# Hybrid trunk: the recurrence's block inversion from 8x8 blocks instead of 16x16, with one more level of doubling on TensorE

## The chip, the core and the metric

One core of one Trainium2 chip runs the whole layer in one launch. The metric is device time in microseconds (us). In the text, PE is TensorE (PEld its weight loads), DVE VectorE, ACT ScalarE, POOL GpSimd and SP SyncE, which here only issues transfers. The engines run their own instruction streams in order and wait for each other with semaphores.

## The reference, cut to what matters

One layer over 256 latent and 256 context tokens, width 2048: a recurrent branch (16 heads of 64, forward and backward), a convolution branch, gates, an output projection, then 16 routed experts. The change lies in the recurrence alone:

```python
def step(S, inp):                       # per head, S is 64x64
    r_t, k_t, v_t, w_t, kk_t, a_t = inp
    sa = jnp.einsum('bhvk,bhk->bhv', S, kk_t)
    S = (S * w_t[:, :, None, :] - sa[..., None] * (kk_t * a_t)[:, :, None, :]
         + v_t[..., None] * k_t[:, :, None, :])
    y = jnp.einsum('bhvk,bhk->bhv', S, r_t) if emit else None
    return S, y
```

The kernel does not step through tokens. It cuts a sequence into chunks of 64 tokens and turns a chunk into matrix products. For that it needs, per chunk and head, the inverse of a 64x64 triangular matrix with a unit diagonal: identity plus the masked products of kk with kk*a.

## The kernel before, in words

**Stages of the trace.** Up to 577 us the input projections and the convolution run. From 577 to 1262 us the recurrence runs, then until 1320 us what is left of the gates, then two projections, and from about 1490 us the experts, whose weights (about 400 MB) come in at the memory's speed to the end. The tiles that hold the first expert weights reuse the recurrence's space, so all of that starts after it.

**The recurrence** works on 16 units: eight pairs of heads, each in two directions. A unit's code is a generator in five segments. Segment 1 makes decays and scaled operands (mostly ACT, POOL and DVE). Segment 2 makes the scores (PE L729, masked by DVE into `AT` at L731 and into `KM` at L734) and transposes `VK` and `KB` on PE (L740). Segment 3 is the inversion. Segment 4 applies the inverse (L857) and forms chunk-to-chunk operators in two PSUM banks, which DVE reads out as `PT` and `RB` (L881, L883). Segment 5 chains the chunks (L890 to L904: PE and ACT in turn) and gives `y`. A hand-written table `ORD` interleaves five units: inversion of unit i+1, segment 4 of unit i, scores of unit i+2, segment 1 of unit i+3, segment 5 of unit i.

**The inversion** handles a unit's 16 matrices (8 chunks, 2 heads) at once, 32x32 blocks on the diagonal first. ACT copies those blocks into `Ab`. DVE selects the 16x16 diagonal blocks with two masked additions into `INP` (L781, L783), transposes to `N` (L785) and does a forward substitution of 14 steps, each a product into `tmp` (L792 or L797, by direction) and an addition into `N` (L800). It transposes back (`OUT` L802), spreads the result (`TT` L805) and transposes it (`T` L808). One level of block doubling makes 32x32 inverses of it: PE multiplies the off-diagonal part `X` (masked by POOL, L777) with `T` (L813: 32 small products, four quadrants of the array side by side), ACT copies to `Q`, PE multiplies with `TT` (L820), DVE subtracts from `T` (L822) and transposes (L824). A second doubling, to 64x64, follows on PE and ACT (L833, L842, into `NT8`); the change does not touch it.

**Filling.** The gates' projections (products L221 to L223 into the PSUM bank "big", 12 for each 256 KB of weights that SP loads as `wraw`, ACT rounds as `whi` and POOL completes as `wlo`, L217) and the modulation products (L271) are handed out to the 16 units by `fills`, at lower priority. A scheduler, with times of its own, sets the order of every engine when the program is built. Filling that finds no place in the recurrence stands behind it.

**Buffers.** Segment 3 takes its tiles from rings: `t1` (three of 8x32 elements), `t2` (three of 16x32), `INP` (one).

Of the kernel before, what the change touches and what calls it, by code (L numbers as in the profile page):

```python
# [86 lines left out]
_n = 0  # L87
for _name, _w in (("ident", 128), ("bones", 128), ("ones", 128), ("mA", 128), ("mM", 128),
                  ("d1", 520), ("iota", 32),
                  ("mq", 2), ("mh", 2), ("ml2", 2), ("id16", 16), ("m16", 64), ("sel", 2), ("selE", 16), ("hsel", 2)):  # L90
    _CON[_name] = (_n, _n + _w)
    _n += _w
NCON = _n
# [2 lines left out]
def shape_constants():  # L96
    c = np.zeros((128, NCON), np.float32)
    p = np.arange(128)

    def put(name, v):  # L100
        a, b = _CON[name]
        c[:, a:b] = v.reshape(128, b - a)

    put("ident", np.eye(128))
    put("bones", (p[:, None] // 64 == p[None, :] // 64) * 1.0)
    put("ones", np.ones((128, 128)))
    s = (p % 64)[:, None]
# [4 lines left out]
    l2 = (p % 32) // 16
    put("ml2", (l2[:, None] == np.arange(2)) * 1.0)
    put("mq", (l2[:, None] == np.arange(2)) * -1.0)
    put("id16", ((p % 16)[:, None] == np.arange(16)) * 1.0)
    m16 = [(l2[:, None] == d) & (np.arange(32)[None, :] // 16 == 1 - d) for d in range(2)]
# [12 lines left out]
def kernel(  # L129
# [179 lines left out]
    with tc.tile_pool(name="st", bufs=1) as st:  # L309
# [52 lines left out]
    with tc.tile_pool(name="p1", bufs=1) as p1:  # L362
# [261 lines left out]
    def rwkv_dir(p, d, Pv, bonr, bon, INP):  # L624
# [148 lines left out]
        Ab8 = rt("Ab", "t1", [8, 32])  # L773
        for z, r in quads:
            act_copy(Ab8[r].rearrange("p (c h) t -> p c h t", h=2), par(AT[r], 1 - z // 2)[..., 32 * (z % 2):32 * (z % 2) + 32])
        X = rt("X", "t1", [8, 32])
        POOL.tensor_tensor(X, Ab8, cst("m16")[:, d * 32:d * 32 + 32][:, None, :].to_broadcast([128, 8, 32]), op=OP.mult)  # L777

        mq, mh, ml2 = cst("mq"), cst("mh"), cst("ml2")
        sel = INP.rearrange("p x u -> p u x")[:, 0:8]  # L780
        DVE.scalar_tensor_tensor(sel, Ab8[:, :, 0:16], mq[:, 0:1], cst("id16")[:, None, :].to_broadcast([128, 8, 16]),  # L781
                                 op0=OP.mult, op1=OP.add)
        DVE.scalar_tensor_tensor(sel, Ab8[:, :, 16:32], mq[:, 1:2], sel, op0=OP.mult, op1=OP.add)  # L783
        N = rt("N", "t2", [16, 32])
        DVE.transpose(N, INP)  # L785
        Nv = N.rearrange("p x (l y) -> p l x y", l=2)
        for j in range(1, 15):
            n, m = j, 15 - j
            tmp = rt("tmp", "tmp", [2 * 56])[:, 0:2 * n * m]
            if d == 0:  # L790
                tv = tmp.rearrange("p (l r s) -> p l r s", l=2, r=m)
                DVE.tensor_tensor(tv, Nv[:, :, j:j + 1, 0:j].to_broadcast([128, 2, m, n]),  # L792
                                  Nv[:, :, j + 1:16, j:j + 1].to_broadcast([128, 2, m, n]), op=OP.mult)
                o = Nv[:, :, j + 1:16, 0:j]
            else:
                tv = tmp.rearrange("p (l s r) -> p l s r", l=2, r=m)
                DVE.tensor_tensor(tv, Nv[:, :, 0:j, j:j + 1].to_broadcast([128, 2, n, m]),  # L797
                                  Nv[:, :, j:j + 1, j + 1:16].to_broadcast([128, 2, n, m]), op=OP.mult)
                o = Nv[:, :, 0:j, j + 1:16]
            DVE.tensor_tensor(o, o, tv, op=OP.add)  # L800
        OUT = rt("OUT", "t2", [16, 32])
# [3 lines left out]
        DVE.tensor_tensor(TT.rearrange("p u (l x) -> p u l x", l=2), outv[:, :, None, :].to_broadcast([128, 8, 2, 16]),  # L805
                          ml2[:, None, :, None].to_broadcast([128, 8, 2, 16]), op=OP.mult)
        T = rt("T", "t1", [8, 32])
        DVE.transpose(T, TT)  # L808
        pq = c8(bank("sb"))
        for i in range(8):  # L810
            tick(0.12)
            for z, r in quads:
                mark["X"] = PE.matmul(pq[r, i, 0:32], X[r, i], T[r, i], start=True, stop=True)  # L813
        Q = rt("Q", "t1", [8, 32])
        act_copy(Q, pq[:, :, 0:32])
        pq = c8(bank("sb"))
        for i in range(8):
            tick(0.12)
            for z, r in quads:
                PE.matmul(pq[r, i, 0:32], TT[r, i], Q[r, i], start=True, stop=True)  # L820
        T2 = rt("T2", "t1", [8, 32])
        DVE.tensor_tensor(T2, T, pq[:, :, 0:32], op=OP.subtract)  # L822
        TT = rt("TT", "t1", [8, 32])
        DVE.transpose(TT, T2)  # L824
# [557 lines left out]
```

## Time and profile before

| what | value |
|---|---|
| median of 3 runs (lowest, highest) | 2432.16 us (2431.11, 2433.72) |
| the profiled execution's own time, and its span | 2433.61 us, 2431.8 us |
| PE busy over the span | 2006.9 us (83%) |
| DVE busy | 1023.9 us (42%) |
| ACT, POOL busy | 763.2 us (31%), 650.8 us (27%) |
| granted PE clock over the span | 0.901 of full speed |
| chain that ended last, over the span: DMA, PE, DVE | 31%, 20%, 6% |

The shares over the span average stages with different limits: transfers at 427 GB/s set the last 900 us, and DVE is hardly busy there. The rows further down are therefore cut to the recurrence. The clock column (PEclk) is a mean of two levels, 1.0 (2.4 GHz) and 0.5 (1.2 GHz). Idle time in front of an instruction carries the name of what ended it.

### The profile page before, as it was taken

How to read it: one execution, taken by the hardware profiler on the slowest of the kernel's cores; microseconds unless marked ns; L12 is line 12 of the kernel's file. 1: busy time of each engine (PE TensorE's matmuls, PEld its weight loads, DVE VectorE, ACT ScalarE, POOL GpSimd, SP SyncE). 2: the span in 40 equal slices, each digit the busy share in tenths (PEclk: the TensorE clock that was granted, in tenths of full speed). 3: DMA queues.
4: the chain of work that ended last, by engine and by line, in shares of the span. 5: the costliest groups of instructions: out<-in, count | busy, mean ns of one | idle time of the engine just before them, and what ended most of it. 6: DMA issues, size and time to landing. Idle time of an engine off the chain costs nothing.

```text
span 2431.8 us, 45085 instructions
## 1 busy us (share of the span) xinstructions
PE 2006.9 (83%) x18730; PEld 1415.9 (58%) x18730; DVE 1023.9 (42%) x2029; ACT 763.2 (31%) x1524; POOL 650.8 (27%) x690
## 2 busy tenths in 40 slices
PE   7998999996877989988798996877777777777765
PEld 3787888894755877767678994433333333333332
DVE  2337888426777787665601543211111111111112
ACT  3254333634545565556443541000000000000002
POOL 1342333336433545445445732000000000000002
PEclk9999999998778999999998998888889889888987
DMA  9958666665213334234256887999999999999995
GB/s 384 343 183 271 216 218 233 202 213 181 60 56 109 125 123 139 96 134 152 97 197 198 280 314 303 427 427 428 428 427 427 428 427 429 427 428 427 428 416 221
DMA packets 145932, 669.94 MB, mean 275 GB/s; under 512 B 17344, under 2 KB 40000, under 8 KB 108608
## 3 DMA queue, kind: packets, MB, share of 16 engines
q1 hardware_dynamic: 128208, 455.49, 50.9%
q10 hardware_dynamic: 17520, 211.58, 20.6%
q8 instruction: 147, 2.41, 0.4%
q14 instruction: 57, 0.47, 0.1%
HBM read 647.28 MB, written 19.73 MB: 274 GB/s over the span
## 4 chain that ended last, share of the span: by engine, by line
DMA 31%; PE 20%; DVE 6%; ACT 3%; POOL 2%; issue 2%; SPq 0%; ACTq 0%; DVEq 0%; POOLq 0%
DMA wx<-in_w_gu 18%; DMA wx<-in_w_dn 10%; PE big L1261 2%; PE rw L1224 2%; DMA wraw<-in_w_in 2%; PE p L1293 2%; DVE N L800 1%; PE rw L1253 1%; PE big L221 1%; PE big L223 1%; PE rw L223 1%; PE big L222 1%; PE rw L221 1%; PE rw L222 1%; POOL wlo L217 1%
## 5 line engine op out<-in xcount | busy, mean ns | idle before, releaser
L217 POOL TENSOR_TENSOR wlo<-wraw,whi 128x512 fp32r<-128x512 f32 x292 | 394.4, 1356 | 517.4 <-ACT whi L146 450.0
L1261 PE MATMUL big<-wx,xse 128*32 128x512 f32 x2048 | 300.1, 721 | 160.3 <-DMA wx<-in_w_gu 158.4
L146 ACT ACTIVATE whi<-wraw 128x512 fp32r<-128x512 f32 x428 | 263.4, 627 | 420.2 <-DMA wraw<-in_w_in 130.0
L221 PE MATMUL big<-hh,whi 128*128 128x256 f32 x912 | 272.7, 299 | 13.6 <-ACT whi L146 6.1
L223 PE MATMUL big<-hh,wlo 128*128 128x256 f32 x912 | 271.0, 298 | 10.1 <-POOL wlo L217 9.9
L1261 PEld LDWEIGHTS big<-wx,xse 128*32 128x32 f32 x2048 | 63.8, 121 | 358.9 <-DMA wx<-in_w_gu 183.6
L222 PE MATMUL big<-hl,whi 128*128 128x256 f32 x912 | 268.1, 294 | 0.0
L1237 POOL TENSOR_TENSOR r<-r 128x256 f32<-128x256 f32 x11 | 8.2, 747 | 922.0 <-ACT r L1233 921.6
L221 PEld LDWEIGHTS big<-hh,whi 128*128 128x128 f32 x912 | 181.7, 199 | 40.0 <-issue 17.7
L223 PEld LDWEIGHTS big<-hh,wlo 128*128 128x128 f32 x912 | 181.6, 199 | 23.2 <-POOL wlo L217 14.1
L1274 ACT ACTIVATE th<-big 128x256 f32<-128x256 f32 x16 | 6.1, 384 | 584.9 <-PE big L1261 472.5
L222 PEld LDWEIGHTS big<-hl,whi 128*128 128x128 f32 x912 | 182.1, 200 | 7.4 <-issue 5.8
L1275 DVE SCALAR_TENSOR_TENSOR th<-th,big 128x256 f32<-128x256 f32 x16 | 6.7, 421 | 408.0 <-ACT th L1274 408.0
L1228 DVE SCALAR_TENSOR_TENSOR x<-rw,modT,x 128x256 f32<-128x256 f32 x256 | 111.3, 479 | 142.1 <-PE rw L1224 142.0
L217 DVE TENSOR_TENSOR wlo<-wraw,whi 128x512 fp32r<-128x512 f32 x136 | 112.7, 834 | 131.0 <-ACT whi L146 122.7
L1224 PE MATMUL rw<-oT,ye 128*128 128x256 f32 x512 | 132.4, 403 | 32.5 <-ACT ye L146 31.7
L223 PE MATMUL rw<-hh,wlo 128*128 128x256 f32 x512 | 149.9, 294 | 6.8 <-POOL wlo L217 6.8
L221 PE MATMUL rw<-hh,whi 128*128 128x256 f32 x512 | 150.3, 296 | 1.5 <-ACT whi L146 1.1
L222 PE MATMUL rw<-hl,whi 128*128 128x256 f32 x512 | 149.0, 293 | 0.0
L463 DVE SCALAR_TENSOR_TENSOR cv<-up,hcw,cv 128x256 f32<-128x256 f32 x240 | 144.6, 608 | 9.5 <-ACT cv L461 2.8
L1224 PEld LDWEIGHTS rw<-oT,ye 128*128 128x128 f32 x512 | 95.2, 196 | 85.9 <-ACT ye L146 72.4
L1253 PEld LDWEIGHTS rw<-oh,xk 128*128 128x128 f32 x1024 | 123.2, 194 | 34.2 <-issue 29.1
(359 smaller groups left out, 3901.4 us busy)
## 6 DMA issues: line engine op xcount, KB each, us to landing
wx<-in_w_gu ACTq DMA_DIRECT2D x66, 2048.0 KB, 39.2
wx<-in_w_gu SPq DMA_DIRECT2D x61, 2048.0 KB, 39.3
wm<-in_w_mod SPq DMA_DIRECT2D x96, 1024.0 KB, 7.2
wraw<-in_w_in SPq DMA_DIRECT2D x300, 256.0 KB, 4.2
wx<-in_w_dn ACTq DMA_DIRECT2D x32, 2048.0 KB, 38.6
wx<-in_w_dn SPq DMA_DIRECT2D x31, 2048.0 KB, 38.1
wraw<-in_w_o SPq DMA_DIRECT2D x64, 256.0 KB, 6.1
wraw<-in_w_co SPq DMA_DIRECT2D x32, 256.0 KB, 3.0
```

The source lines that it names most:

```text
L146: return ACT.activation(o, i, AF.Copy, scale=scale)
L217: (POOL if LO[0] < LO[1] else DVE).tensor_tensor(lo, raw, hi, op=OP.subtract)
L221: PE.matmul(o, hi, xh, start=start, stop=False, skip_group_check=True)
L222: PE.matmul(o, hi, xl, start=False, stop=False, skip_group_check=True)
L223: PE.matmul(o, lo, xh, start=False, stop=stop, skip_group_check=True)
L463: DVE.scalar_tensor_tensor(o, up[:, :, j:j + 64], hcw[:, i * KC + j:i * KC + j + 1], o, op0=OP.mult, op1=OP.add)
L800: DVE.tensor_tensor(o, o, tv, op=OP.add)
L1224: PE.matmul(pq[:, 256 * q:256 * q + 256], y[:, 128 * q:128 * q + 128], oT, start=True, stop=True)
L1228: DVE.scalar_tensor_tensor(x, pq[:, 256 * q:256 * q + 256], modT[:, 5, k + q, 0:1], x, op0=OP.mult, op1=OP.add)
L1253: PE.matmul(pxs[:, k], xk[:, s, k], oh[:, s, e], start=(s == 0), stop=(s == 1))
L1261: PE.matmul(pg[32 * j:32 * j + 32, :], xs[:, k, :], w[:, a:a + 512], start=(k == 0), stop=(k == KD - 1))
L1293: PE.matmul(pd[32 * j:32 * j + 32, u], aT[:, 128 * b + 32 * j:128 * b + 32 * j + 32], w[:, 2 * j + b, u], start=(b == 0), stop=(b == 1))
```

## The change

Substitution stops at 8x8 blocks: 6 steps of two DVE instructions instead of 14, on four blocks side by side where there were two (24 to 48 elements instead of 28 to 112). `INP`, `N` and `OUT` shrink to 8x32, so the two transposes handle 256 elements instead of 512, and the selection is four masked additions of 64 elements instead of two of 128. The doubling level on PE runs twice, first with mask `m8` (8 to 16), then with `m16` (16 to 32): 64 more small products for each unit, one more ACT copy, one more DVE subtraction and transpose, one more POOL mask multiplication. The ring `t1` gets five tiles instead of three and takes `N` and `OUT` too; `X` gets a ring of two for itself. The products and the order outside segment 3 are written as before.

```diff
-        X = rt("X", "t1", [8, 32])
-        POOL.tensor_tensor(X, Ab8, cst("m16")[...], op=OP.mult)
+        XS = []
+        for n in ("m8", "m16"):
+            XS.append(rt("X", "tx", [8, 32]))
+            POOL.tensor_tensor(XS[-1], Ab8, cst(n)[...], op=OP.mult)
...
-        for j in range(1, 15):
-            n, m = j, 15 - j
+        for j in range(1, 7):
+            n, m = j, 7 - j
...
-        pq = c8(bank("sb"))
-        for i in range(8):
-            tick(0.12)
-            for z, r in quads:
-                mark["X"] = PE.matmul(pq[r, i, 0:32], X[r, i], T[r, i], start=True, stop=True)
+        for X in XS:
+            pq = c8(bank("sb"))
+            for i in range(8):
+                for z, r in quads:
+                    PE.matmul(pq[r, i, 0:32], X[r, i], T[r, i], start=True, stop=True)
+            Q = rt("Q", "t1", [8, 32])
+            act_copy(Q, pq[:, :, 0:32])
...
+            T2 = rt("T2", "t1", [8, 32])
+            DVE.tensor_tensor(T2, T, pq[:, :, 0:32], op=OP.subtract)
+            TT = rt("TT", "t1", [8, 32])
+            DVE.transpose(TT, T2)
+            T = T2
```

The scheduler builds every engine's order anew. In the changed kernel, line numbers above L112 are 3 higher, and behind the inversion 6 higher.

First DVE, between the second and the third inversion (`T` from `sb` is a level's subtraction, `INP` the next unit's selection). Before, from the one subtraction to the next unit's substitution:

```order
L822 TENSOR_TENSOR T_6432<-T,sb 128x256
L824 STREAM_TRANSPOSE TT<-T_6432 128x256
L692 TENSOR_TENSOR KB<-kp,Wy 128x4x2x64
L692 TENSOR_TENSOR KB<-ta,Wy 128x4x128
L708 TENSOR_TENSOR rk<-p_6647,VK 128x256
L781 SCALAR_TENSOR_TENSOR INP<-Ab,C 128x8x16
L783 SCALAR_TENSOR_TENSOR INP<-Ab,C,INP 128x8x16
L785 STREAM_TRANSPOSE N<-INP 128x512
L792 TENSOR_TENSOR tmp<-N 128x28
```

The level ends there, and three instructions of later units lie between it and the next selection. Now:

```order
L827 TENSOR_TENSOR T_6464<-T,sb 128x256
L829 STREAM_TRANSPOSE TT<-T_6464 128x256
L734 TENSOR_TENSOR AT<-rw,C 128x4x64 x2
L647 SCALAR_TENSOR_TENSOR VK<-Pv,V,VK 128x4x64 x2
L679 SCALAR_TENSOR_TENSOR Wp<-dp,C 128x520
L679 SCALAR_TENSOR_TENSOR Wy<-di,C 128x520
L827 TENSOR_TENSOR T_6536<-T_6464,sb 128x256
L829 STREAM_TRANSPOSE TT<-T_6536 128x256
L685 SCALAR_TENSOR_TENSOR Wy<-di,Wy 128x520
L695 TENSOR_TENSOR KB<-kp,Wy 128x4x2x64
L695 TENSOR_TENSOR KB<-ta,Wy 128x4x128
L787 SCALAR_TENSOR_TENSOR INP<-Ab,C 128x8x8
```

There are two subtractions, and six instructions of later units (scores, operands, scans) stand between them.

Then PE, right behind the last chunk product of the fifth unit. Before, with filling ("big") between the recurrence's products:

```order
L271 MATMUL big<-wm,slp 32x512
L740 MATMUL rw<-C,VK 128x128 x4
L271 MATMUL big<-wm,slp 32x512 x3
L222 MATMUL big<-ssp,whi 128x256
L223 MATMUL big<-ssp,wlo 128x256
L221 MATMUL big<-ssp,whi 128x256
L222 MATMUL big<-ssp,whi 128x256
L223 MATMUL big<-ssp,wlo 128x256
L729 MATMUL rw<-VK,KB 128x64 x4
L842 MATMUL sb<-TT,Q 32x32 x16
L729 MATMUL rw<-VK,KB 128x64 x4
```

Nine of these products are filling. Now:

```order
L910 MATMUL gn<-RB,Z 64x64 x8
L819 MATMUL sb<-T_9708,X 32x32 x32
L743 MATMUL rw<-C,VK 128x128 x6
L732 MATMUL rw<-VK,KB 128x64 x4
L896 MATMUL gn<-VU,KM 64x64 x5
L825 MATMUL sb<-Q,TT 32x32 x32
L732 MATMUL rw<-VK,KB 128x64 x4
L743 MATMUL rw<-C,KB 128x128 x8
L896 MATMUL gn<-VU,KM 64x64 x4
L839 MATMUL sb<-T_9780,AT 32x32 x16
L896 MATMUL gn<-VU,KM 64x64 x5
```

Here the second level's products (L819, then L825) stand where filling stood. Counted in the order, the products of L221 to L223 between the first scores and the last unit's last product are 1510 before and 1380 now, those of L271 108 and 100; the rest stands behind the recurrence. By the end of units 2, 3, 4, 5 and 6 the units had 35, 4, 79, 110 and 55 products of L221 to L223 each before, and have 20, 27, 2, 52 and 24 now.

## Rows read from the trace of the kernel before

**Rows 1.** Busy time by stretch: length; PE, PEld, DVE, ACT, POOL (instructions); PEclk; DMA; GB/s.
```profile
...
577.00:767.00 190.00, 140.52 (x2062) 114.82 (x2060) 142.75 (x273) 91.59 (x196) 80.34 (x98) 0.76 0.25 77
842.00:1110.00 268.00, 241.22 (x3617) 194.17 (x3613) 191.38 (x396) 154.30 (x337) 131.21 (x142) 0.94 0.38 123
1262.00:1320.00 58.00, 48.30 (x317) 42.15 (x316) 6.19 (x10) 22.86 (x40) 33.70 (x28) 0.85 0.65 204
sum 743.00, PE 630.09 PEld 517.27 DVE 460.07 ACT 389.43 POOL 351.68; mean PE 126.02 PEld 103.45 DVE 92.01 ACT 77.89 POOL 70.34
```

**Rows 2.** Groups on DVE, 577 to 1262 us: shapes, count | busy us, mean ns | idle.
```profile
...
L800 DVE TENSOR_TENSOR N<-N,tmp 128x28 f32<-128x28 f32 (+6 forms) x224 | 100.2, 447 | 6.6
L792 DVE TENSOR_TENSOR tmp<-N 128x28 f32<-128x28 f32 (+6 forms) x112 | 56.0, 500 | 3.2
L797 DVE TENSOR_TENSOR tmp<-N 128x28 f32<-128x28 f32 (+6 forms) x112 | 49.4, 441 | 3.2
L785 DVE STREAM_TRANSPOSE N<-INP 128x512 f32<-128x512 f32 x16 | 11.4, 711 | 0.6
L781 DVE SCALAR_TENSOR_TENSOR INP<-Ab,C 128x128 f32<-128x128 f32 x16 | 11.4, 710 | 22.4 <-ACT Ab L146 22.4
L802 DVE STREAM_TRANSPOSE OUT<-N 128x512 f32<-128x512 f32 x16 | 11.3, 709 | 0.4
L783 DVE SCALAR_TENSOR_TENSOR INP<-Ab,C,INP 128x128 f32<-128x128 f32 x16 | 7.6, 474 | 0.5
L808 DVE STREAM_TRANSPOSE T<-TT 128x256 f32<-128x256 f32 x16 | 7.1, 443 | 0.6
L822 DVE TENSOR_TENSOR T<-T,sb 128x256 f32<-128x256 f32 x16 | 6.7, 416 | 5.0 <-PE sb L820 4.9
...
```

**Rows 3.** One line's instructions (min/median/max ns, first and last start, forms).
```profile
L800 DVE TENSOR_TENSOR N<-N,tmp x224: 178/263/1420, 581.5 to 1196.0; 128x28 f32<-128x28 f32 x16, 128x72 f32<-128x72 f32 x16, 128x100 f32<-128x100 f32 x16, 128x112 f32<-128x112 f32 x16
...
```

**Rows 4.** Timeline, DVE and POOL, 895 to 899 us (start, length).
```profile
...
895.28 2.50 POOL L217 TENSOR_TENSOR wlo<-wraw,whi 128x512 fp32r<-128x512 f32 x2
895.42 1.20 DVE L792 TENSOR_TENSOR tmp<-N 128x52 f32<-128x52 f32 x1
896.65 1.19 DVE L800 TENSOR_TENSOR N<-N,tmp 128x52 f32<-128x52 f32 x1
897.88 0.23 DVE L792 TENSOR_TENSOR tmp<-N 128x72 f32<-128x72 f32 x1
...
```

**Rows 5.** Waits of PE, 577 to 1262 us: total, times, longest.
```profile
...
PE rw L729 <- DVE KB L692: 19.5, 3, 8.9
PE rw L729 <- DVE RB L883: 18.0, 4, 7.5
PE sb L813 <- DVE T L808: 11.3, 5, 6.5
PE gn L895 <- DVE PT L881: 6.8, 1, 6.8
...
```

**Rows 6.** PE busy with lines L813 and L820 alone (two answers), 577 to 1262 us.
```profile
577.00:1262.00 685.00, 16.31 (x1024) 13.08 (x1024) 0.88 0.36 116
...
577.00:1262.00 685.00, 13.63 (x1024) 11.15 (x1024) 0.88 0.36 116
```

**Rows 7.** Timeline, PE, one unit's products of L813, run together.
```profile
...
690.34 0.75 PE L813 MATMUL sb<-T,X 32*32 32x32 f32 x64
...
```

**Rows 8.** Busy time with the filling's bank "big" alone, in the recurrence and behind it.
```profile
...
577.00:1262.00 685.00, 269.67 (x1705) 206.70 (x1704) 6.06 (x15) 13.41 (x32) 0.88 0.36 116
1262.00:1320.00 58.00, 46.04 (x301) 39.92 (x300) 0.00 (x0) 2.45 (x6) 0.85 0.65 204
```

**Rows 9.** Chain of waits, 842 to 1262 us: share of the stretch by line.
```profile
by line: DVE N L800 8.3%; PE big L221 6.4%; PE big L223 6.0%; PE big L222 6.0%; DVE tmp L797 5.4%; PE rw L729 5.2%; DMA wm<-in_w_mod 5.2%; DVE tmp L792 4.6%; PE big L271 3.7%; issue 3.4%; PE rw L740 2.9%; DMA wraw<-in_w_in 2.8%; PE gn L895 
...
```

**Rows 10.** A unit with little filling (676 to 726 us) and one with much.
```profile
...
676.00:726.00 50.00, 32.28 (x558) 27.16 (x557) 37.98 (x85) 19.29 (x45) 16.70 (x23) 0.73 0.18 52
803.00:842.00 39.00, 36.23 (x620) 32.14 (x616) 28.84 (x61) 23.38 (x51) 16.47 (x18) 0.96 0.37 115
...
```

More of the change, by code (lines that the diff above doesn't have):

```diff
@@ L89 @@
                   ("d1", 520), ("iota", 32),
-                  ("mq", 2), ("mh", 2), ("ml2", 2), ("id16", 16), ("m16", 64), ("sel", 2), ("selE", 16), ("hsel", 2)):
+                  ("mq", 4), ("mh", 2), ("ml4", 4), ("id8", 8), ("m8", 64), ("m16", 64), ("sel", 2), ("selE", 16), ("hsel", 2)):
     _CON[_name] = (_n, _n + _w)
@@ L111, in shape_constants @@
     put("mh", (s // 32 == np.arange(2)) * -1.0)
[L112 to L116, printed above, removed]
+    l4 = ((p % 32) // 8)[:, None]
+    put("ml4", (l4 == np.arange(4)) * 1.0)
+    put("mq", (l4 == np.arange(4)) * -1.0)
+    put("id8", ((p % 8)[:, None] == np.arange(8)) * 1.0)
+    t4 = np.arange(32)[None, :] // 8
+    m8 = [(l4 // 2 == t4 // 2) & (l4 % 2 == d) & (t4 % 2 == 1 - d) for d in range(2)]
+    put("m8", np.concatenate(m8, 1) * 1.0)
+    m16 = [(l4 // 2 == d) & (t4 // 2 == 1 - d) for d in range(2)]
     put("m16", np.concatenate(m16, 1) * 1.0)
@@ L613 @@
     rw = rw_stack.enter_context(tc.tile_pool(name="rw", bufs=1))
-    BUF = dict(VK=1, KB=1, a2=7, rm=2, bon=3, RB=3, WCk=3, t4=2, VU=3, KBt=3, t2=3, NT8=2, t1=3, c2=3,
+    BUF = dict(VK=1, KB=1, a2=7, rm=2, bon=3, RB=3, WCk=3, t4=2, VU=3, KBt=3, t2=3, NT8=2, t1=5, tx=2, c2=3,
                ys=3, Pv=1, km=1, kn=1, gw=2, bonr=1, tmp=2)
@@ L775, in rwkv_dir @@
             act_copy(Ab8[r].rearrange("p (c h) t -> p c h t", h=2), par(AT[r], 1 - z // 2)[..., 32 * (z % 2):32 * (z % 2) + 32])
-        X = rt("X", "t1", [8, 32])
-        POOL.tensor_tensor(X, Ab8, cst("m16")[:, d * 32:d * 32 + 32][:, None, :].to_broadcast([128, 8, 32]), op=OP.mult)
-        mq, mh, ml2 = cst("mq"), cst("mh"), cst("ml2")
-        sel = INP.rearrange("p x u -> p u x")[:, 0:8]
-        DVE.scalar_tensor_tensor(sel, Ab8[:, :, 0:16], mq[:, 0:1], cst("id16")[:, None, :].to_broadcast([128, 8, 16]),
-                                 op0=OP.mult, op1=OP.add)
@@ L783, in rwkv_dir @@
-        DVE.scalar_tensor_tensor(sel, Ab8[:, :, 16:32], mq[:, 1:2], sel, op0=OP.mult, op1=OP.add)
-        N = rt("N", "t2", [16, 32])
+        XS = []
+        for n in ("m8", "m16"):
+            XS.append(rt("X", "tx", [8, 32]))
+            POOL.tensor_tensor(XS[-1], Ab8, cst(n)[:, d * 32:d * 32 + 32][:, None, :].to_broadcast([128, 8, 32]), op=OP.mult)
+        mq, mh, ml4 = cst("mq"), cst("mh"), cst("ml4")
+        sel = INP.rearrange("p x u -> p u x")[:, 0:8]
+        for l in range(4):
+            DVE.scalar_tensor_tensor(sel, Ab8[:, :, 8 * l:8 * l + 8], mq[:, l:l + 1],
+                                     sel if l else cst("id8")[:, None, :].to_broadcast([128, 8, 8]),
+                                     op0=OP.mult, op1=OP.add)
@@ L785, in rwkv_dir @@
+        N = rt("N", "t1", [8, 32])
         DVE.transpose(N, INP)
-        Nv = N.rearrange("p x (l y) -> p l x y", l=2)
-        for j in range(1, 15):
-            n, m = j, 15 - j
-            tmp = rt("tmp", "tmp", [2 * 56])[:, 0:2 * n * m]
+        Nv = N.rearrange("p x (l y) -> p l x y", l=4)
+        for j in range(1, 7):
+            n, m = j, 7 - j
+            tmp = rt("tmp", "tmp", [4 * 12])[:, 0:4 * n * m]
             if d == 0:
[L791 to L794, printed above, removed]
-            else:
[L796 to L799, printed above, removed]
+                tv = tmp.rearrange("p (l r s) -> p l r s", l=4, r=m)
+                DVE.tensor_tensor(tv, Nv[:, :, j:j + 1, 0:j].to_broadcast([128, 4, m, n]),
+                                  Nv[:, :, j + 1:8, j:j + 1].to_broadcast([128, 4, m, n]), op=OP.mult)
+                o = Nv[:, :, j + 1:8, 0:j]
+            else:
+                tv = tmp.rearrange("p (l s r) -> p l s r", l=4, r=m)
+                DVE.tensor_tensor(tv, Nv[:, :, 0:j, j:j + 1].to_broadcast([128, 4, n, m]),
+                                  Nv[:, :, j:j + 1, j + 1:8].to_broadcast([128, 4, n, m]), op=OP.mult)
+                o = Nv[:, :, 0:j, j + 1:8]
@@ L800, in rwkv_dir @@
             DVE.tensor_tensor(o, o, tv, op=OP.add)
-        OUT = rt("OUT", "t2", [16, 32])
+        OUT = rt("OUT", "t1", [8, 32])
         DVE.transpose(OUT.rearrange("p x u -> p x u"), N)
@@ L804, in rwkv_dir @@
         TT = rt("TT", "t1", [8, 32])
-        DVE.tensor_tensor(TT.rearrange("p u (l x) -> p u l x", l=2), outv[:, :, None, :].to_broadcast([128, 8, 2, 16]),
-                          ml2[:, None, :, None].to_broadcast([128, 8, 2, 16]), op=OP.mult)
+        DVE.tensor_tensor(TT.rearrange("p u (l x) -> p u l x", l=4), outv[:, :, None, :].to_broadcast([128, 8, 4, 8]),
+                          ml4[:, None, :, None].to_broadcast([128, 8, 4, 8]), op=OP.mult)
         T = rt("T", "t1", [8, 32])
         DVE.transpose(T, TT)
-        pq = c8(bank("sb"))
-        for i in range(8):
-            tick(0.12)
-            for z, r in quads:
-                mark["X"] = PE.matmul(pq[r, i, 0:32], X[r, i], T[r, i], start=True, stop=True)
[L814 to L824, printed above, removed]
+        for X in XS:
[5 more added lines that the diff above has]
+            act_copy(Q, pq[:, :, 0:32])
+            pq = c8(bank("sb"))
+            for i in range(8):
+                for z, r in quads:
+                    PE.matmul(pq[r, i, 0:32], TT[r, i], Q[r, i], start=True, stop=True)
+            T2 = rt("T2", "t1", [8, 32])
[3 more added lines that the diff above has]
+            T = T2
         NT8 = rt("NT8", "NT8", [8, 64])
@@ L910 @@
     POOL.tensor_copy(con_idb[64:128], ident[64:128, 64:128])
-    INP = rw.tile([128, 16, 32], F32, name="INP")
+    INP = rw.tile([128, 8, 32], F32, name="INP")
     POOL.memset(INP, 0.0)
```

## The prediction

> **What bounds the kernel now.** I read the table by stretch first, cut where the recurrence begins and ends. From 577 to 1320 us, 743 us, PE is busy for 630.1 us, so it idles for 112.9 [rows 1]. Two regimes are to be seen there. From 842 to 1110 us PE is busy for 241 of 268 us at a granted clock of 0.94, DVE for 191: PE is nearly full. From 577 to 767 us PE is busy for 140.5 of 190 us at 0.76, DVE for 142.8: the units there hold little filling, and the chain over DVE sets the pace. Everything behind 1320 us has the same instructions in the changed kernel and starts when this stretch ends, so I take the change of the stretch as the change of the time. Next come the groups on DVE [rows 2]: substitution (L800, L792, L797) is by far its largest work, 100.2 + 56.0 + 49.4 = 205.6 us in 448 instructions, 459 ns each, although the median of L800 is 263 ns and the longest takes 1420 [rows 3]. The timeline says why: the two that start at 895.42 and 896.65 us take 1.20 and 1.19 us while POOL runs two `wlo` subtractions, 2.50 us long; the next, on more elements and with POOL silent, takes 0.23 [rows 4]. Last come PE's waits: 19.5 us for `KB`, 18.0 for `RB`, 11.3 for `T`, 6.8 for `PT`, 55.6 us in all [rows 5]. All four come out of the DVE queue in which substitution stands, so these are the waits that a shorter one can end.
>
> **The change, part by part.** I make the sum on PE: what it gets to do more, and which of its waits end.
>
> *DVE.* A unit's substitution costs 205.6 / 16 = 12.85 us now. The 12 instructions that remain have 24 to 48 elements; undisturbed, 28 elements take 178 ns at the least [rows 3] and 72 take 230 [rows 4], so I take 200 ns, and per instruction the same delay by POOL as now, 459 - 263 = 196 ns: 12 x 0.396 = 4.75 us, 8.1 less. The transposes `N` and `OUT` fall from 0.71 to the 0.443 us of L808, which has their new size [rows 2]: 0.53 less. Selection takes 0.71 + 0.47 = 1.18 us now; the three later additions of 64 elements lie between 0.18 (the shortest tiny operation) and 0.47 (128 elements) [rows 2, 3], nearest to neither, so 0.35: 0.71 + 3 x 0.35 = 1.76, 0.58 more. From `INP` to `OUT` a unit now costs 12.85 + 1.18 + 1.42 = 15.5 us; 8.05 of that goes, 52%. The second level gives back 0.416 + 0.443 = 0.86 us (L822 and L824, which has L808's size) [rows 2].
>
> *PE's work.* The first level, L813 and L820, keeps PE busy for 16.31 + 13.63 = 29.9 us [rows 6], with pauses inside; 64 records run together take 0.75 us [rows 7], which gives 2 x 16 x 0.75 = 24 us. The second level issues the same products. I take **+29.9 us** (24 to 29.9): PE is the fuller engine, and in thin units, where it could hide, the pauses are the longest.
>
> *PE's waits that end.* Of the 55.6 us I take the share of the inversion's DVE time that goes, 52%: **-28.9 us**. At one end nothing goes (the wait moves on to the next late operand), at the other all 55.6.
>
> *New waits.* The second level waits for DVE's first subtraction and then for ACT's copy, and PE's queue behind it waits too: scores of the next units, products with `PT`, filling. The nearest row is the same wait one level earlier, L813 for `T`, 11.3 us [rows 5]. I take **+11.3 us**, from 0 (the scheduler put enough in between) to 22.6 (both waits fully). On DVE the subtraction has six instructions of later units behind the first one, so there its wait is covered at the place shown.
>
> *Order.* The order leaves 130 products of L221 to L223 and 8 of L271 (two records each, so 146 records) for the stretch behind the recurrence. In the recurrence a record of the filling costs 269.67 / 1705 = 0.158 us of PE; behind it 301 took 58 us, 0.193 each [rows 1, 8]: the loads of `wraw`, ACT's `whi` and POOL's `wlo` pace it there. Moving them costs 146 x 0.035 = **+5.1 us**; if PE idles where they stood, all of 146 x 0.193 = 28. SP's loads move along with them.
>
> *At nothing:* POOL's second mask, a multiplication of 256 elements, and ACT's second copy. POOL is busy for 131 and ACT for 154 of 268 us [rows 1]; without that cover the mask would hold up the `wlo` behind it. The larger rings only take waits away.
>
> Sum: 29.9 - 28.9 + 11.3 + 5.1 = **+17.4 us**. The profiled execution took 2433.61 us, 1.8 more than its span, so it would become 2451.0. It lies 1.45 us above the median, so I say **2449.6 us** (+0.7%). All terms at their best give 24 - 55.6 = -31.6 (2400.6), all at their worst 29.9 + 22.6 + 28 = +80.5 (2512.7).
>
> **The rivals.**
>
> *DVE sets the pace throughout* (faster). In the chain of waits from 842 to 1262 us substitution holds 8.3 + 5.4 + 4.6 = 18.3% [rows 9], 76.9 us, more than any other work. With 8.1 / 12.85 = 63% of it gone, 48.4 us go. A second level puts 2 x 0.75 + 0.416 + 0.443 [rows 2, 7] and a copy of about 0.42 (ACT's, taken as long as DVE's of that size) on the chain, 2.78 us for each of 16 x 420 / 685 = 9.8 units, 27.3. That is -21.1 in 420 us, -34.4 in 685; with the +5.1, -29.3 and **2402.9 us**. For it speaks that the chain runs over DVE in the dense units too; against it, that PE idles for only 27 of 268 us there and has to take 29.9 us more. It decides if PE's idle time in the stretch falls from 112.9 below 112.9 - 29.9 - 29.3 = 54 us.
>
> *The delays by POOL don't go with the instructions* (slower). If POOL's operations simply hold up whichever DVE instruction comes next, only the undisturbed time is saved: 16 x 0.263 + 12 x 0.063 + 0.53 - 0.58 = 4.9 of 15.5 us, 32%, so 17.6 us of waits instead of 28.9: **2460.9 us**. In its favour: both long instructions in rows 4 end with a POOL operation. The Trainium skill states this as a rule: on the page "SBUF — State Buffer", in "SBUF: two separate sides", DVE operations with two SBUF inputs and GpSimd operations share a pair of ports by an exclusive lock, held for a whole instruction, and the loser blocks. By that rule the sum is the one just given; the trace's 1.20 us beside the 0.23 agrees with it.
>
> *Thin units lose the clock* (slower). The unit from 676 to 726 us, with little filling, took 50 us at a clock of 0.73; the one from 803 to 842, well filled, 39 us at 0.96 [rows 10]. The new order thins out units 4, 5 and 6 and two near the end as well. If these five each lose part of that 11 us, which for want of a row I put at six tenths, 6.5, instead of getting faster, the sum rises by 32.5 to **2482 us**. Against it: substitution, which made the thin units slow, is what shrinks.
>
> *Gains and costs cancel* (no change): about 46 us of the waits go, the rest as in the sum: **2432 us**.
>
> **How the numbers follow.** The forecast gets 0.32, the POOL rival 0.12, the clock rival 0.15, all slower, 0.59 together; cancelling 0.15; DVE sets the pace 0.26. What a measurement can tell from no change is about 0.2%, 4.9 us. So faster 0.26, same 0.15, slower 0.59. The range leaves out about a tenth on each side: its low end, 2412, takes in the nearer half of the DVE rival, its high end, 2482, the clock rival. Both signs hold much of the chance; the forecast's own range is 2437 to 2462.
>
> **What would show it.** In the profile after, substitution's groups should add up to about 16 x 4.75 = 76 us, with a mean near 0.4 us; near 0.5 would speak for the POOL rival, 0.25 against any delay. L819 and L825 should double PE's time for the level, to about 60 us. PE's waits for `KB`, `RB` and `PT` should halve, and a wait of the second level for the subtraction should be there. The recurrence should end at about the same time as now, and the filling behind it should take some 28 us longer than the 58 now. If the recurrence ends more than 35 us earlier, the DVE rival is right and my place for the bound wrong; if the clock between 676 and 900 us is below 0.85, the clock rival.

## The result, and the profile after

The changed kernel takes 2462.41 us (median of 4 runs, 2458.81 to 2463.46), the kernel before 2431.64 (4 runs beside it). The ratio is 1.0125, with a 95% interval of 1.0108 to 1.0143: about 31 us slower, where +17.4 us was forecast and the range ended at 2482. The profiled execution took 2462.65 us, 29.0 more than that of before, with a span of 2460.9.

The table by stretch, cut where units end (the stretch now ends at 1351 us; columns as in [rows 1]):

```profile
...
577.00:678.00 101.00, 75.55 (x1356) 63.62 (x1358) 71.56 (x122) 50.71 (x110) 53.09 (x63) 0.83 0.26 80
678.00:841.00 163.00, 149.64 (x2956) 121.18 (x2948) 97.71 (x214) 94.19 (x212) 55.07 (x75) 0.81 0.23 70
841.00:1171.00 330.00, 290.71 (x4802) 235.44 (x4798) 180.47 (x341) 177.69 (x378) 173.46 (x179) 0.90 0.39 123
1171.00:1268.00 97.00, 84.71 (x1325) 69.78 (x1322) 17.51 (x44) 43.78 (x100) 36.12 (x31) 0.95 0.42 136
1268.00:1351.00 83.00, 69.17 (x470) 59.71 (x469) 8.07 (x11) 31.00 (x56) 47.30 (x39) 0.88 0.67 215
sum 774.00, PE 669.77 PEld 549.72 DVE 375.33 ACT 397.36 POOL 365.03; mean PE 133.95 PEld 109.94 DVE 75.07 ACT 79.47 POOL 73.01
```

The stretch grew from 743 to 774 us. PE is busy in it for 669.8 us (630.1 before), and idle for 104.2 (112.9). DVE fell from 460.1 to 375.3. So DVE has far less to do, but PE's idle time fell by only 8.7 us while its busy time grew by 39.7. Unit 6 ends at 841 us, 40 us earlier than before; the next seven take 330 us to 1171 (before 268, from 881 to 1149), where filling (the products for the gates) that was put off comes in; behind the recurrence the filling takes 83 us, where it took 58 [rows 1].

The groups on DVE that answer to [rows 2], 577 to 1268 us (line numbers are 3 higher up to the inversion, then 6):

```profile
...
L806 DVE TENSOR_TENSOR N<-N,tmp 128x24 f32<-128x24 f32 (+2 forms) x96 | 35.0, 365 | 3.1
L787 DVE SCALAR_TENSOR_TENSOR INP<-Ab,C,INP 128x64 f32<-128x64 f32 x48 | 31.4, 655 | 1.6
...
L798 DVE TENSOR_TENSOR tmp<-N 128x24 f32<-128x24 f32 (+2 forms) x48 | 20.3, 422 | 1.4
...
L803 DVE TENSOR_TENSOR tmp<-N 128x24 f32<-128x24 f32 (+2 forms) x48 | 16.8, 351 | 1.6
...
L787 DVE SCALAR_TENSOR_TENSOR INP<-Ab,C 128x64 f32<-128x64 f32 x16 | 13.2, 828 | 28.0 <-ACT Ab L149 28.0
L827 DVE TENSOR_TENSOR T<-T,sb 128x256 f32<-128x256 f32 x32 | 13.0, 408 | 52.5 <-PE sb L825 52.5
...
L791 DVE STREAM_TRANSPOSE N<-INP 128x256 f32<-128x256 f32 x16 | 7.1, 446 | 0.6
L808 DVE STREAM_TRANSPOSE OUT<-N 128x256 f32<-128x256 f32 x16 | 7.1, 443 | 0.7
...
```

Substitution (L798, L803, L806) is 20.3 + 16.8 + 35.0 = 72.1 us in 192 instructions, 375 ns each. Selection (L787), 19.0 us in all before [rows 2], is 44.6 us now.

PE's waits, the answer to [rows 5]:

```profile
...
PE sb L819 <- DVE T L814: 43.7, 13, 9.9
...
PE rw L732 <- DVE KB L695: 4.2, 1, 4.2
...
PE gn L901 <- DVE PT L887: 1.0, 1, 1.0
...
PE rw L732 <- DVE RB L889: 0.5, 1, 0.5
...
```

`KB`, `RB` and `PT`, 44.3 us before, are down to 5.7. The wait of the level for `T` (L814, the first level's) went from 11.3 to 43.7 us. For the second level no row has L819 released by the subtraction (L827). PE's time with the level's two lines alone, the answer to [rows 6]:

```profile
577.00:1268.00 691.00, 31.40 (x2048) 25.48 (x2048) 0.88 0.34 106
...
577.00:1268.00 691.00, 30.05 (x2048) 24.54 (x2048) 0.88 0.34 106
```

### The profile page after: what moved, and what is told of

Same layout as the page of the kernel before. It is cut to its first block, busy times and chain, and to the rows that moved or that the text cites. A ratio compares the mean times of both kernels' runs of the same rounds, so it can differ in the third digit from the quotient of the medians.

```text
span 2460.9 us, 49006 instructions
## 1 busy us (share of the span) xinstructions
PE 2052.6 (83%) x20778; PEld 1450.4 (59%) x20778; DVE 938.5 (38%) x1837; ACT 770.2 (31%) x1540; POOL 664.4 (27%) x706
## 4 chain that ended last, share of the span: by engine, by line
DMA 29%; PE 22%; DVE 4%; POOL 2%; ACT 2%; issue 2%; SPq 1%; ACTq 0%; DVEq 0%; POOLq 0%
DMA wx<-in_w_dn 15%; DMA wx<-in_w_gu 10%; PE rw L1230 3%; DMA wraw<-in_w_in 2%; PE p L1299 2%; PE rw L1259 2%; PE big L1267 2%; PE gn L1299 1%; PE rw L226 1%; PE rw L224 1%; PE rw L225 1%; POOL wlo L220 1%; PE big L225 1%; PE big L224 1%; PE big L226 1%
## 5 line engine op out<-in xcount | busy, mean ns | idle before, releaser
L220 DVE TENSOR_TENSOR wlo<-wraw,whi 128x512 fp32r<-128x512 f32 x136 | 112.9, 836 | 121.2 <-ACT whi L149 108.2
L1259 PEld LDWEIGHTS rw<-oh,xk 128*128 128x128 f32 x1024 | 123.7, 195 | 35.0 <-issue 28.3
```

The lines of the kernel that those rows point to most:

```text
L220: (POOL if LO[0] < LO[1] else DVE).tensor_tensor(lo, raw, hi, op=OP.subtract)
L1259: PE.matmul(pxs[:, k], xk[:, s, k], oh[:, s, e], start=(s == 0), stop=(s == 1))
```

## The experiments

For every run the table cuts out the stretch from the first product of the scores to the first product behind the filling (before: 568.4 to 1320.2 us). Ahead of it the kernels shown spend 563 to 573 us, behind it, up to PE's last product, 1098 to 1105 (e1b 1115), so this stretch holds nearly all differences. Its columns come from one profiled execution each, within 3 us of the median of the runs except for e1b and e11, whose profiled executions were 9 and 10 us slower than their medians. "At 1.2 GHz" is the time of the stretch at the lower level of PE's clock: length times 2 x (1 - granted clock), summed over 20 equal parts. "Behind" counts the products of L221 to L223 that the order leaves for behind the recurrence.

| kernel | us; ratio to before (95%) | stretch | PE busy | PE idle | at 1.2 GHz | behind |
|---|---|---|---|---|---|---|
| before | 2431.64 | 751.8 | 638.7 | 113.1 | 178.9 | 288 |
| changed | 2462.41; 1.0125 (1.0108 to 1.0143) | 783.5 | 679.2 | 104.3 | 195.0 | 418 |
| e1 level alone | 2455.44; 1.0101 (1.0073 to 1.0130) | 782.6 | 663.2 | 119.4 | 168.2 | 240 |
| e1b products off the chain | 2578.97; 1.0622 (1.0591 to 1.0652) | 889.2 | 700.0 | 189.2 | 351.2 | 1 |
| e2 substitution alone | 2391.80; 0.9846 (0.9826 to 0.9866) | 710.7 | 612.7 | 98.0 | 135.7 | 274 |
| e3 changed, lag 650 | 2460.34; 1.0135 (1.0099 to 1.0170) | 781.2 | 688.5 | 92.7 | 157.0 | 298 |
| e4 changed, no second mask | 2439.74; 1.0024 (1.0004 to 1.0044) | 760.3 | 654.3 | 106.0 | 160.5 | 322 |
| e5 substitution alone, lag 0 | 2421.99; 0.9955 (0.9937 to 0.9973) | 733.0 | 657.8 | 75.2 | 144.4 | 113 |
| e6 before, lag 0 | 2441.73; 1.0044 (1.0021 to 1.0067) | 753.9 | 639.7 | 114.2 | 172.6 | 113 |
| e7 changed, lag 0 | 2423.44; 0.9970 (0.9951 to 0.9990) | 737.6 | 646.1 | 91.5 | 100.3 | 58 |
| e8 changed, masks on ACT | 2419.68; 0.9967 (0.9949 to 0.9986) | 737.8 | 639.5 | 98.4 | 127.6 | 300 |
| e9 the same, lag 0 | 2436.30; 1.0022 (0.9999 to 1.0044) | 752.1 | 669.2 | 82.9 | 134.6 | 82 |
| e10 level alone, lag 0 | 2478.69; 1.0222 (1.0187 to 1.0257) | 798.3 | 680.1 | 118.2 | 199.6 | 107 |
| e11 changed, dense products | 2467.37; 1.0167 (1.0137 to 1.0197) | 794.9 | 687.0 | 107.9 | 158.2 | 347 |

The kernel before measured 2430 to 2432 us beside each group. The first theory, called PE, was the forecast's: PE's work is paid in full and the shorter DVE chain returns little. The rival, called order, was that the place of the filling makes the difference.

**e1, level alone.**

```diff
+X0 = [[ident[r, 32 * ((z + 1) % 4):32 * ((z + 1) % 4) + 32]] * 8 for z, r in quads]
+X1 = [[X[r, i] for i in range(8)] for z, r in quads]
+for XX in (X0, X1):
...
```

> The kernel before (substitution on 16x16) with a second doubling level added whose left operand is zero, so that it subtracts nothing: 2 x 64 more products in each unit, ACT's copy, DVE's subtraction and transposition, all in the chain; POOL's mask is left out, and one ring of tiles is one larger, one one smaller. Theory PE (PE is the fuller engine, its work is paid in full, 31.5 us as in the changed kernel, and little of the level's latency): 2463 to 2473 us. Theory order (what costs is that filling is put off to later units and behind the recurrence, and elsewhere the chain over DVE paces): the chain grows by 2.8 us in each of 16 units, 45 us, 2477 us, however the filling lies.

The left operand `X0` holds zeros. 25 us more, below both forecasts. The work is there (PE busy +24.5), the latency is not: PE's idle time grew by 6.3 us only.

**e1b, the products off the chain.**

```diff
+pq = c8(bank())
+for k in range(2):
+    for i in range(8):
+        for z, r in quads:
+            PE.matmul(pq[r, i, 32 * k:32 * k + 32], ident[r, r], T2[r, i], start=True, stop=True)
```

> The kernel before with 2 x 64 products of the level's size added in each unit behind the first level, into a bank that nobody reads: the work of the second level without its chain. Theory PE: 24 to 31.5 us more, 2456 to 2463 us. Theory order (PE idles for 113 us of the stretch and these products can stand in it): 2432 to 2437 us. This kernel's order leaves 1 filling product behind the recurrence, where the kernel before has 288 and the changed one 418; if the place of the filling by itself were worth the 28 us by which the stretch grew, it would gain on that side too, 2410 us or less.

149 us more: both theories missed, and the kernel doesn't measure what it was made for. PE is 76 us longer idle and 172 us longer at 1.2 GHz. The products take one of the three banks through which the recurrence's own products rotate, which may be the reason; it was not followed up. All it says of the filling's place is that one product left behind the recurrence does not by itself make a kernel fast.

**e2, substitution alone.**

```diff
-for n in ("m8", "m16"):
+for n in ("m16",):
```

> The changed kernel without the new level (8 to 16), which is left out of the computation: the shorter substitution alone. Theory PE: the waits for KB, RB and PT go, but most of it comes back as a wait for the first level's T, as in the changed kernel (idle time down by 8.7 us): 2421 to 2431 us. Theory order, with the chain over DVE as the pace: 7.3 us less in each unit, 117 us, of which the chain's share of 0.61 gives 72: 2360 us.

38 us less, halfway between. The parts by themselves give -38 and +25, together -13; the changed kernel has both and stands at +31. **Some 44 us are in neither part**, and they became the question. Its waits, with the same columns:

```profile
...
PE sb L819 <- DVE T L814: 43.3, 9, 10.6
PE rw L732 <- DVE KB L695: 6.9, 3, 4.9
...
```

The wait for `T` is as long as in the changed kernel, and e1 has 7.9 us of it: at this lag it comes with the shorter substitution, not with the second level. This fits a DVE that is less full in front of later units: those units' operands are there in time, and what PE then meets first is the inversion's own `T`.

**e3, the changed kernel with the filling earlier.** The filling's instructions stand behind the others by a lag in the scheduler's priority.

```diff
-LOWP = 1500
+LOWP = 650
```

> The changed kernel with the filling's lag in priority at 650 instead of 1500: the same instructions, 298 filling products behind the recurrence instead of 418 (288 in the kernel before), and units 5 to 15 hold 94 to 134 each instead of 16 to 169. Theory PE: the work is the same, only the surcharge of the filling behind the recurrence goes (about 5 us): 2455 to 2464 us. Theory order: the 28 us go, 2434 us.

No change: with as much filling behind the recurrence as before, the time stays. What the forecast called order, the surcharge of the filling behind the recurrence, is not the loss. Nor does the clock alone decide here: 38 us less of the stretch run at 1.2 GHz, for the same time.

**e4, no second mask.**

```diff
-for n in ("m8", "m16"):
+for n in ("m16",):
...
+X0 = [[ident[r, 32 * ((z + 1) % 4):32 * ((z + 1) % 4) + 32]] * 8 for z, r in quads]
+X1 = [[XS[0][r, i] for i in range(8)] for z, r in quads]
+for XX in (X0, X1):
```

> The changed kernel whose new level has a left operand of zeros, so that POOL's multiplication with the new mask is not there; the level's products, copy, subtraction and transposition stay, but subtract nothing (the 8 to 16 step is thereby left out of the computation). The substitution alone gave 39 us less and the level alone 25 us more than before, but the two together 31 us more: 44 us are missing. Theory mask (POOL's two masks in a row run beside the selection on DVE and hold up both; the level alone had no such mask): 2462 - 44 = 2418 us. Theory order (the place of the filling decides how much of PE's time falls into the low clock): up to 10 us on either side, 2450 to 2472 us.

23 us less than the changed kernel, half of the 44, and between the two forecasts. But 34 us less of it run at 1.2 GHz as well, so the run does not tell the mask from the order.

**e5, e6, e7: lag 0** (`LOWP = 0`) for the substitution alone, the kernel before and the changed kernel.

> The shorter substitution alone (the new level left out of the computation) with the filling's lag in priority at 0 instead of 1500: 113 filling products behind the recurrence, 39 to 140 in each unit from the third on. Theory order: part of the 39 us was a favourable place of the filling; against the kernel before at the same lag 10 to 25 us less. Theory parts (each part has its price whatever the order): 38 us less than the kernel before at the same lag.

> The kernel before with the filling's lag at 0: 113 filling products behind the recurrence instead of 288, units from the third on hold 52 to 139. Theory order: the order of the kernel before happens to be a good or a bad one, and 10 to 30 us go either way, 2400 to 2460 us. Theory parts: PE's work is the same, 2422 to 2436 us.

> The changed kernel with the filling's lag at 0: 58 filling products behind the recurrence instead of 418, units from the third on hold 74 to 142. Theory order (the thin units 2 to 6 kept PE in the low clock, 177 us of its busy time in the stretch against 100 with the substitution alone): the clock comes back and the time falls below 2445 us, and against the kernel before at lag 0 it is 15 us or less. Theory parts: 2455 to 2465 us.

The same edit makes the kernel before 10 us slower, the substitution alone 30 us slower, and the changed kernel **39 us faster**, so that it beats the kernel before (0.9970, 0.9951 to 0.9990). At lag 0 the change is worth -18 us, at lag 1500 +31. That is the theory order; that each part has its price whatever the order has fallen. The wait for `T` belongs to the order too: at lag 0 the kernel before has 28.7 us of it with the long substitution, e5 29.4 with the short one. In e6:

```profile
...
PE sb L813 <- DVE T L808: 28.7, 9, 8.9
...
```

How filling and clock go together is seen in units 4 and 6 of the changed kernel and of e7 (busy time with the filling's bank alone, its records, and the granted clock). The changed kernel:

```profile
...
743.40:773.60 30.20, 3.83 (x18) 0.72 0.36 122
811.60:841.20 29.60, 5.46 (x24) 0.66 0.04 11
```

and the same two units at lag 0:

```profile
...
751.70:787.30 35.60, 17.81 (x113) 0.95 0.34 110
834.20:874.50 40.30, 18.10 (x131) 1.00 0.38 128
```

18 and 24 filling records go with a clock of 0.72 and 0.66, 113 and 131 with 0.95 and 1.00. It is no strict rule (unit 3 of the changed kernel has 35 records at 0.95, unit 12 has 88 at 0.75), and it is not where the time was lost: with little filling in them the changed kernel's two units are shorter. Over the whole stretch the same products keep PE busy for 33 us less in e7 than in the changed kernel, and PE idles for 13 us less.

**e8, e9: masks on ACT**, at lag 1500 and 0.

```diff
-for n in ("m8", "m16"):
-    XS.append(rt("X", "tx", [8, 32]))
-    POOL.tensor_tensor(XS[-1], Ab8, cst(n)[...], op=OP.mult)
+XS = XP[d]
+for t in (1 - d, 3 - d):
+    l = 2 * (t // 2) + d
+    act_copy(XS[0][:, :, 8 * t:8 * t + 8], Ab8[:, :, 8 * t:8 * t + 8], cst("ml4")[:, l:l + 1])
+act_copy(XS[1][:, :, 16 - 16 * d:32 - 16 * d], Ab8[:, :, 16 - 16 * d:32 - 16 * d], cst("ml2")[:, d:d + 1])
```

> The changed kernel with both masked copies made by ACT (three scaled copies of the columns that are not zero, into tiles that are cleared once) instead of POOL's two multiplications; the lag of the filling stays at 1500, and units 3 to 6 hold 15, 9, 42 and 29 filling products (changed kernel: 27, 2, 52, 24). Theory mask (POOL's masks beside DVE's selection cost the 23 us by which the kernel without the second mask was faster): 2430 to 2442 us, selection on DVE at 0.45 us instead of 0.70. Theory order (thin units decide, the mask does not): 2452 to 2468 us.

> The same at lag 0: 82 filling products behind the recurrence, units 3 to 15 hold 70 to 140. Theory mask: 2423 - 23 = 2400 us. Theory order: 2415 to 2430 us, as the changed kernel at lag 0.

`XP` holds four tiles, cleared once. e8 is 43 us faster than the changed kernel and 0.33% faster than the kernel before, below both forecasts; with e7 it is the fastest kernel that computes everything. e9 is above both forecasts, 13 us slower than e7. The selection of e8 (577 to 1244 us) and of e9 (577 to 1307):

```profile
...
L789 DVE SCALAR_TENSOR_TENSOR INP<-Ab,C,INP 128x64 f32<-128x64 f32 x48 | 18.1, 377 | 1.7
...
L789 DVE SCALAR_TENSOR_TENSOR INP<-Ab,C 128x64 f32<-128x64 f32 x16 | 6.4, 397 | 27.2 <-ACT Ab L150 27.2
...
```

```profile
...
L789 DVE SCALAR_TENSOR_TENSOR INP<-Ab,C,INP 128x64 f32<-128x64 f32 x48 | 31.4, 655 | 1.4
...
L789 DVE SCALAR_TENSOR_TENSOR INP<-Ab,C 128x64 f32<-128x64 f32 x16 | 9.9, 618 | 6.2 <-ACT Ab L150 6.2
...
```

e8 needs 24.5 us for it where the changed kernel needs 44.6, but e9, which has no mask on POOL either, needs 41.3. With one mask on POOL, e2 needs 35.1 and e4 39.3. By these rows it is not the masks alone that count, but all that POOL does beside the selection. One unit each (start, length; two answers for DVE and POOL where both are shown): the changed kernel with both masks beside the selection, e8 with POOL silent, e9 with three `wlo` subtractions beside it.

```profile
...
691.75 0.81 DVE L787 SCALAR_TENSOR_TENSOR INP<-Ab,C 128x64 f32<-128x64 f32 x1 [1.58 <-ACT Ab L149]
692.59 1.30 DVE L787 SCALAR_TENSOR_TENSOR INP<-Ab,C,INP 128x64 f32<-128x64 f32 x3
...
691.79 1.23 POOL L782 TENSOR_TENSOR X<-Ab,C 128x256 f32<-128x256 f32 x2 [3.30 <-ACT Ab L149]
```

```profile
...
1002.60 0.33 DVE L789 SCALAR_TENSOR_TENSOR INP<-Ab,C 128x64 f32<-128x64 f32 x1 [2.22 <-ACT Ab L150]
1002.97 1.09 DVE L789 SCALAR_TENSOR_TENSOR INP<-Ab,C,INP 128x64 f32<-128x64 f32 x3
...
```

```profile
...
769.38 1.35 DVE L789 SCALAR_TENSOR_TENSOR INP<-Ab,C 128x64 f32<-128x64 f32 x1
...
770.94 2.70 DVE L789 SCALAR_TENSOR_TENSOR INP<-Ab,C,INP 128x64 f32<-128x64 f32 x3
...
768.87 4.25 POOL L221 TENSOR_TENSOR wlo<-wraw,whi 128x512 fp32r<-128x512 f32 x3
```

Four selections take 2.11 us beside the two masks, 1.42 with POOL silent and 4.05 beside `wlo`. By the first two the masks cost DVE an estimated 0.69 us in a unit, 11 us in 16; the rest of the 20 us between the changed kernel and e8 is other work on POOL, which the order puts there or elsewhere. The thin units of e8 are as thin as in the changed kernel (15, 9, 42 and 29 products in units 3 to 6). So neither theory holds alone, and what the masks cost in time is not shown.

**e10, level alone at lag 0** (e1 with `LOWP = 0`).

> The kernel before with the new level alone (its left operand zero) at lag 0: 107 filling products behind the recurrence. At lag 0 the substitution alone gave 20 us less than before and both parts together 18 us less. Theory order (at an order with filling in every unit the level's products cost next to nothing, 1 to 8 us): 2443 to 2450 us. Theory PE (the products are paid in full, and the pair at lag 0 gains elsewhere): 2465 to 2475 us.

37 us more than e6, above both forecasts: beside the long substitution the level is paid in full at this order too. So e1 and e10 (+25 and +37) agree in sign and roughly in size; it is the pair that does not add up. At lag 1500 it stands 44 us above the sum of its parts, at lag 0 (-20 and +37 against -18) some 35 below.

**e11, dense products in the thin units.**

```diff
+def dense(pq):
+    for k in range(10 if 1 <= 2 * p + d <= 6 else 0):
+        PE.matmul(pq[:, :, 32:64], slh[:, 0, 0:128], slh[:, 1, 0:256], start=True, stop=True)
...
 PE.matmul(pq[r, i, 0:32], X[r, i], T[r, i], start=True, stop=True)
+dense(pq)
```

> The changed kernel (lag 1500) with 40 useless products of the filling's size in each of the units 2 to 7 (240 in all, 0.118 us each at the full clock, 28 us), ten behind each of the level's four groups of products, into columns that nobody reads. Theory clock (thin units run at 1.2 GHz because only small products stand in them: 0.66 of the clock from 812 to 841 us with PE busy for 28.4 of 29.6 us): the granted clock between 678 and 841 us rises from 0.81 to above 0.90, which gives back 25 to 35 us: 2450 to 2470 us. Theory work (PE's records are what costs, the clock is a bystander): 28 us more and the chain 5 us longer in six units, 2490 to 2515 us, the clock below 0.87.

The time falls into the range of the theory clock, 5 us above the changed kernel, but not for its reason: the clock between 678 and 841 us is 0.85 (0.81 in the changed kernel), not above 0.90. Units 2 to 7, changed kernel and e11:

```profile
...
677.60:878.60 201.00, 184.60 (x3450) 0.84 0.28 89
```

```profile
...
676.10:935.00 258.90, 230.80 (x3953) 0.85 0.25 82
```

They became 58 us longer at about the same clock. The stretch behind them became 43 us shorter, 429 instead of 473, at 0.94 instead of 0.90. As much filling is left there (1488 records of its bank, 1492 in the changed kernel), but not the same work: 5799 records of PE in all instead of 6114, since 159 records of bank `rw` (scores, transposes, operators) and 144 of bank `sb` (inversion) were already done. So it is no evidence that dense products hold the clock up; how much of the 43 us is work moved forward, and how much the clock, it does not tell.

**All runs together.** Twelve kernels carry none, one or both parts (all but e1b and e11). Four numbers fitted to their stretches describe them with a scatter of 8.8 us: 754.4 us for the kernel before, -10.8 (standard error 7.0) for the substitution, +33.5 (5.6) for the level, and 0.56 (0.12) for each us more at 1.2 GHz. The largest miss is e3, 16.3 us. Without the clock's column the scatter is 16.4. The two kernels outside the fit come out at 765.5 + 28.3 = 793.8 (e11, with the dense products at the full clock; measured 794.9) and 850.2 + 25.4 = 875.6 (e1b, with its products' busy time; measured 889.2). For the change it gives 22.7 us from the two parts and 16.1 x 0.56 = 9.0 from the clock, 31.7 in all. It is a description found afterwards, from one profiled execution each: the time at 1.2 GHz goes with the order, no run set it alone (e11 was meant to), and a kernel that is slow for another reason may idle into the lower clock. Executions of one kernel, whose order is the same, show less. In the 88 executions of the thirteen kernels below the first row, compared within each kernel, 0.01 less granted clock over the span (49 us more at 1.2 GHz) goes with 7 us more, 0.15 for each us. That clock takes in all that stands behind the stretch, so this does not disprove the 0.56, but it does not bear it out either.

## Why the prediction was right, point by point

*The bound.* Right: 679.2 of 783.5 us PE is busy, 87%, and 85 to 90% in all kernels but e1b (79%). DVE has 85 us less to do and PE idles for 8.7 us less, so "DVE sets the pace throughout" is wrong for this order.

*DVE.* Substitution was put at 76 us and 0.396 us each, and measured 72.1 and 0.375, so for this order the share of delay that POOL adds was right and the POOL rival (0.5) is out. That is in part luck: the other eight kernels with the same 192 instructions need 0.40 to 0.48 us each (e2, e3 and e11 0.46 to 0.48). The POOL rival's time, 2460.9, is near the measured one without its mark being there. Selection was put at 1.76 us a unit and took 44.6 / 16 = 2.79. The term took the row of one mask on POOL. Beside the two masks alone a unit takes 2.11 us, and the rest of the 2.79 comes from `wlo` and other work on POOL. "At nothing" for POOL's second mask was wrong, though on DVE it is small: both masks together cost it an estimated 0.69 us in a unit, and with none on POOL the selection took 24.5 us in e8 and 41.3 in e9. The Trainium skill has the rule, on the page "SBUF — State Buffer", in "SBUF: two separate sides": an instruction of DVE with two inputs in SBUF and one of POOL hold a shared pair of ports in turn, each for its whole length. The four selections' 2.11 us beside the masks, 1.42 with POOL silent and 4.05 beside `wlo` agree with it.

*PE's work.* Put at +29.9 us; L819 and L825 measure 31.4 + 30.1 against 29.9 before, +31.5, and the fit prices the level at +33.5 (5.6).

*Waits that end, new waits.* Put at -28.9 and +11.3, together -17.6. The old waits fell further, by 38.6. The new wait came at the wrong place: not at the second level for the subtraction (no such row), but at the first level for `T`, +32.4. The two sum to -6.2, PE's idle time says -8.7, and the fit -10.8 (7.0) for the substitution. This term was the largest miss of the sum, 7 to 11 us. The step that failed is the share: 52% of the waits were said to go, without asking what PE meets next when the operands are in time. It meets the inversion's own result, which e2 shows without the second level (43.3 us). At lag 0 the kernel before meets it too (28.7 us), so how many waits move on to `T` depends on the order.

*Order.* Behind the recurrence it cost 25 us, as put (28), and the recurrence ends 6 us later, nearly as put. But over the stretch the 2028 records of the filling's bank cost PE 320.7 us, 320.5 before, so the surcharge of 5.1 us is not there, and e3 moves that filling back in and gains nothing. That is not what makes an order dear or cheap: with both parts in, e3, e7, e8 and e9 lie between 2420 and 2460 us.

*The clock rival* had its chance at 0.15 and its mark below 0.85 between 676 and 900 us; the clock stands at 0.85 there, 0.86 before. Its mechanism is there (rows of units 4 and 6 above), its price is not: the stretch has 16 us more at 1.2 GHz, some 9 us by the fit, where it was given 32.5, and the thin units still became shorter, 33 us instead of 41. The forecast's sum left this out.

*Where the 31 us come from.* By the rows, PE is busy for 40.5 us more in the stretch and idle for 8.7 less. Of the 40.5 the two lines of the level make 31.5; the recurrence's other products (banks `rw` and `gn`), in the same number, take 288.2 us instead of 277.0; the filling's bank adds 0.2 (records of different banks overlap, so these do not add up exactly). That the forecast had nothing for these 11 us, and took too much off for the waits, is its miss. By the fit it reads 17.4 + 9.0 (clock) + 6.8 (waits, from -17.6 to -10.8) = 33.2, less the 5.1 of order, plus 3.6 on the level, 31.7 in all; since the changed kernel is one of the twelve that were fitted, this is no second proof. That the lower clock made those products dearer is not shown by a run.

So the sign and the mechanism held for this order, and only for it: at lag 0, or with the masks on ACT, the same two parts are 0.3% faster than the kernel before. What in an order decides, beyond the time at 1.2 GHz that goes with it, stays open.

## What to carry to other kernels

Ask of each wait that an edit ends what the waiting engine meets next; here 38.6 us of waits became 32.4 us of another one. Where a scheduler orders anew, an edit is timed together with the order that it happens to get: run both kernels at two or three settings of the knob that places the independent work before believing a per cent, since here one setting made the same change -18 us and another +31. And work on POOL is not free while DVE runs many short operations beside it: here four selections took 1.42 us with POOL silent, 2.11 beside two masks and 4.05 beside `wlo`.

## What the runs showed of the hardware

PE's clock can be at its lower level while PE is never idle by its records. The changed kernel from 794 to 834 us (length, PE busy, clock), where no record of the filling stands between 802 and 826:

```profile
...
794.00:802.00 8.00, 5.65 (x137) 0.95 0.43 132
802.00:810.00 8.00, 8.00 (x122) 0.50 0.01 4
810.00:818.00 8.00, 8.00 (x180) 0.50 0.01 2
818.00:826.00 8.00, 8.00 (x106) 0.50 0.01 2
826.00:834.00 8.00, 7.09 (x79) 0.63 0.12 34
```

For 24 us PE is busy all the time, with products of 32 to 128 rows by 32 to 128 columns, and stays at 0.50 (1.2 GHz); ahead of 802 us it had been idle for 2.35 of 8 us, and the clock is back at 1.00 from 832 us, after filling has come in again. The same line's products on both sides, 771 to 782 us and 803 to 819 us (two answers):

```profile
...
L732 PE MATMUL rw<-VK,KB x32: 272/272/373, 771.2 to 781.9; 64*128 64x128 f32 x16, 64*128 64x64 f32 x16
...
L732 PE MATMUL rw<-VK,KB x32: 417/418/578, 803.1 to 819.3; 64*128 64x128 f32 x16, 64*128 64x64 f32 x16
...
```

The first run at a granted clock of 1.00 (2.4 GHz) and take 272 ns, the second at 0.50 (1.2 GHz) and take 418. The Trainium skill, "TensorE: Matmul & The Clock Gate", in "Part 1: The HAM clock gate", puts the lower level down to an idle PE and the upper one to a busy one; that PE is back at the upper level while it works without a pause is not what these rows show. Busy time is modelled from the records, so what the array itself did in those 24 us stays open.
